# A hybrid decoder layer on one core: the residual sum ahead of the second-norm scaling, and x chunks projected in three pieces instead of four

## The chip, the cores and the metric

The kernel runs on one core of a Trainium2 chip. The metric is the device time of one execution in microseconds; before the change the median of three runs was 953.03 us (952.98 to 953.38). The engines of the core are TensorE (PE, its weight loads shown apart as PEld), VectorE (DVE), ScalarE (ACT), GpSimd (POOL) and SyncE (SP), each with its own queue of instructions. DMA transfers are issued from the queues of SP and POOL.

## What is computed

One layer, 1024 tokens with 16 meta tokens in front (1040 columns), model width 1024, FFN width 4096. The reference, cut:

```python
u = rmsnorm(h, g_pre_mix)
q, k, v, x_rec, y_rec = split(u @ w_in)       # 512, 128, 128, 512, 512
a_out = rg_lru(conv4(x_rec)) * gelu(y_rec)    # 8 blocks of 64, gates r and i
b_out = window_attention_with_sinks(q, k, v)  # 8 heads, window 128
h = h + rmsnorm(concat(b_out, a_out) @ w_out, g_post_mix)
f = rmsnorm(h, g_pre_ffn)
h = h + rmsnorm(relu(f @ w_ff1)**2 @ w_ff2, g_post_ffn)
```

In `rg_lru` two gates per channel come from block-diagonal 64x64 matrices: `r = sigmoid(x w_a + b_a)`, `i = sigmoid(x w_x + b_x)`, then `a = exp(-8 r softplus(-lam))`, and `h_t = a_t h_(t-1) + sqrt(1 - a_t^2) i_t x_t` over the tokens.

## The kernel before

Channels lie on the 128 partitions and tokens along the free axis until the output projection, where tokens turn to the partitions. Every float32 product is made of two rounded halves: `split` takes the high part on ACT (L96; on DVE, L98, when it is told to) and the low part on DVE (L99), and `mm3` (L125, L130, L131) issues three matmuls, high x high, high x low, low x high. The FFN, from about 345 us on, uses a scheme with fewer block products; the change does not touch it.

The instructions of each engine stand in an order that a scheduler fixes when the kernel is built: it follows the order of the program with priorities, and `behind(name, ins)` adds an order (no semaphore) between two instructions of one engine. `deferred` lowers the priority of what it encloses.

The stretches that matter here, in time:

- **Attention with fills, about 90 to 190 us.** Two passes of four quarters make scores (L628, L632 into `ps_s`), a softmax, transposes (L678 into `ps_pt`) and the product with v (L696 into `ps_o`). Between them PE is filled with projections of the remaining weight chunks, in the order x0, q2, x1, q3, x2, x3, y0, y1, then y2 and y3. `project(w, pieces, sink)` takes a piece of columns at a time: a bank `ps_acc` (there are two), 24 matmuls (8 k-slices x 3), then `sink`. For x the pieces are `ALL`, four of 272, 256, 256 and 256 columns, and the sink is an ACT copy (L490). For q and y they are `REAL2`, two of 512; the y sink is a DVE copy (L751). A convolution (`conv`) follows each x chunk.
- **Gates.** `gates(c)`, for the four chunks c of 128 channels: for three column pieces of 348, 348 and 344, six matmuls with 64 rows (L818): three for r and i each, on the upper and the lower 64 rows, into banks of `ps_s`, `ps_pt` or `ps_o`. ACT then takes the sigmoids (L82). `gather` (L832 to L835, with a copy on POOL, L833) brings the halves together.
- **Recurrence.** `decay` (exponential and tanh on ACT), `recur` (square root on ACT, two DVE products L850 and L851, a DVE scan L852), gelu of y on ACT, and `rec_out` (DVE product L857 and the split). It goes for chunks 0 and 1 first, then for 2 and 3. `load_wo` and `split_wo` bring the rows of `w_out` in between. The y projection gives PE work meanwhile.
- **Output projection, from about 226 us.** `out_mm(t, po, kcs)` for eight token tiles t of 128, two banks of 512 columns, k-slices kc 0 to 3 (attention), 4 and 5 (chunks 0 and 1), 6 and 7 (chunks 2 and 3). For tiles 0 to 3 the slices are taken in three rounds (0 to 3 for all, 4 and 5 for all, then 6 and 7 tile by tile); tiles 4 to 7 take all eight at once.
- **Norms of a tile.** `out_norm(t, po)`: sums of squares on ACT, the factor on POOL (L176), the scaling with the gain on DVE, DVE residual sum `h + xr` (L954), a DMA of h to the output, sum of squares on ACT, a second factor on POOL, and a DVE scaling into `xr` (L959). `u2_tiles` (L971 transposes on PE into `ps_o`, evictions L976 on DVE and L982 on ACT) makes the FFN's input from `xr`; it is called for tile 0 when t is 4.

Of the kernel before, what the change touches and what calls it, by code (L numbers as in the profile page):

```python
# [12 lines left out]
ALU = mybir.AluOpType  # L13
# [24 lines left out]
def hybrid_layer(  # L38
# [6 lines left out]
    nc = tc.nc  # L45
# [12 lines left out]
    def slot(tag, shape, dt=F32):  # L58
        uid[0] += 1
        return slab.tile(shape, dt, tag=tag, name=f"{tag}{uid[0]}", bufs=bufs[tag])  # L60

    def pair(tag, shape):
        return slot(tag, shape, F32R), slot(tag, shape, F32R)

    def bank(tag, shape=(P, 512)):
        uid[0] += 1
        return ps.tile(list(shape), F32, tag=tag, name=f"ps_{tag}{uid[0]}")
# [26 lines left out]
    def split(hi, lo, src, eng=None):  # L94
        if eng is None:
            nc.scalar.copy(hi, src)  # L96
        else:
            eng.tensor_copy(hi, src)  # L98
        low = nc.vector.tensor_tensor(lo, src, f32(hi), op=ALU.subtract).ins  # L99
        mark[0] = low.name  # L100
        return low
# [4 lines left out]
    def behind(name, *inss):  # L106
        for ins in inss:
            tc.add_manual_dep(
                ins, name,
                mybir.DependencyInfo(  # L110
                    mybir.DependencyClass.NoSync, mybir.DependencyReason.DATA
                ),
                reason="order",
            )
# [8 lines left out]
    def mm3(dst, lhs, rhs, start, stop, after=None):  # L123
        (lh, ll), (rh, rl) = lhs, rhs
        ins = nc.tensor.matmul(  # L125
            dst, lh, rh, start=start, stop=False, skip_group_check=True
        ).ins
        if after:
            behind(after, ins)
        nc.tensor.matmul(dst, lh, rl, start=False, stop=False, skip_group_check=True)  # L130
        last_mm[0] = nc.tensor.matmul(  # L131
            dst, ll, rh, start=False, stop=stop, skip_group_check=True
        ).ins.name
# [33 lines left out]
    def rstd_of(ssq_parts, n=P):  # L167
        ms = small.tile([P, 1], F32, name="ms", tag="ms")
        if len(ssq_parts) == 1:
            nc.gpsimd.tensor_scalar(ms[:n], ssq_parts[0], EPS, None, op0=ALU.add)  # L170
        else:
            nc.vector.scalar_tensor_tensor(
                ms[:n], ssq_parts[0], EPS, ssq_parts[1], op0=ALU.add, op1=ALU.add
            )
        rs = small.tile([P, 1], F32, name="rs", tag="rs")
        last_pow[0] = nc.gpsimd.tensor_tensor(  # L176
            rs[:n], ms[:n], half_pow[:n], op=ALU.pow
        ).ins.name
        return rs[:n]
# [85 lines left out]
    def project(w, pieces, sink):  # L265
        wh, wl = w
        for t0, n in pieces:
            acc = bank("acc")
            for kc in range(KC):
                uh, ul = u[kc]  # L270
                mm3(
                    acc[:, :n], (wh[:, kc, :], wl[:, kc, :]),
                    (uh[:, t0 : t0 + n], ul[:, t0 : t0 + n]),
                    kc == 0, kc == KC - 1,
                )
            sink(acc[:, :n], t0, n)
# [10 lines left out]

    ALL = [(0, 272), (272, 256), (528, 256), (784, 256)]
    REAL2 = [(16, 512), (528, 512)]

# [175 lines left out]
    def new_q():  # L468

        q = pair("b", [P, T])  # L470

        def sink_q(acc, t0, n):
            c = slice(t0 - NMETA, t0 - NMETA + n)
            for h in range(2):
                r = HALF[h]
                nc.scalar.activation(q[h][r, c], acc[r], AF.Copy, scale=-(HD ** -0.5))
            for h in range(2):
                r, o = HALF[h], HALF[1 - h]
                nc.vector.scalar_tensor_tensor(  # L479
                    q[h][o, c], acc[r], -(HD ** -0.5), f32(q[h][r, c]),  # L480
                    op0=ALU.mult, op1=ALU.subtract,
                )

        return q, sink_q

    def new_x(tag="d"):
        xr = slot(tag, [P, TT])

        def sink_x(acc, t0, n):
            nc.scalar.copy(xr[:, t0 : t0 + n], acc)  # L490

        return xr, sink_x
# [224 lines left out]
    def conv(c, xr, tag="d"):  # L717
        y = slot(tag, [P, TT])
        nc.vector.tensor_scalar(
            y, xr, prm[:, c, 3:4], prm[:, c, 4:5], op0=ALU.mult, op1=ALU.add  # L720
        )
        for k in (2, 1, 0):
            s = 3 - k
            nc.vector.scalar_tensor_tensor(
                y[:, s:], xr[:, : TT - s], prm[:, c, k : k + 1], y[:, s:],
                op0=ALU.mult, op1=ALU.add,
            )
        xc[c] = y
# [3 lines left out]
    def fill_q(j):  # L732
        def run(w):
            q, sink = new_q()
            project(w, REAL2, sink)
            qs[j] = q
        return run

    def fill_x(c):
        def run(w):  # L740
            xr, sink = new_x()
            project(w, ALL, sink)
            conv(c, xr, "b" if c == 3 else "d")
        return run

    def fill_y(c):
        def run(w):
# [5 lines left out]

            project(w, REAL2, sink)
            ys[c] = y
# [49 lines left out]
    def gates(c):  # L805
        ch, cl = pair("b", [P, TT])
        split(ch, cl, xc[c])


        z = [slot("c", [P, TT]) for _ in range(2)]  # L810
        for t0, n in ((0, 348), (348, 348), (696, 344)):
            acc = []
            for s in range(2):
                flip[0] += 1
                acc.append(bank(("s", "pt", "o")[flip[0] % 3]))
            for k, (a, b) in enumerate(((0, ch), (0, cl), (1, ch))):
                for s in range(2):
                    nc.tensor.matmul(  # L818
                        acc[s][:, :n], gw[HALF[s], a, c, :], b[HALF[s], t0 : t0 + n],
                        start=k == 0, stop=k == 2, skip_group_check=True,  # L820
                    )
            for s in range(2):
                lut(
                    z[s][:, t0 : t0 + n], acc[s][:, :n], AF.Sigmoid,
                    bias=prm[:, c, 5 + s : 6 + s],
                )
        rg[c] = z
# [106 lines left out]
    def out_banks(t):  # L934
        tag = ("pt", "o", "acc", "s", "pt", "acc", "s", "pt")[t]
        return [bank(tag), bank(tag)]

    def out_norm(t, po):
        xr = slot("d", [P, D])
        nc.sync.dma_start(xr, x[t * P : (t + 1) * P, :])  # L940
        h = slot("raw", [P, D])
        ssq = [small.tile([P, 1], F32, name=f"sq{n}", tag=f"sq{n}") for n in range(2)]
        for n in range(2):
            c = slice(512 * n, 512 * n + 512)
            nc.scalar.activation(
                h[:, c], po[n], AF.Square, scale=RMS_SC, accum_out=ssq[n]
            )
        rs = rstd_of(ssq)
        for n in range(2):
            c = slice(512 * n, 512 * n + 512)  # L950
            nc.vector.scalar_tensor_tensor(
                h[:, c], po[n], rs, gmix_b[:, c], op0=ALU.mult, op1=ALU.mult
            )
        nc.vector.tensor_tensor(h, h, xr, op=ALU.add)  # L954
        nc.sync.dma_start(out[t * P : (t + 1) * P, :], h)
        ssq2 = small.tile([P, 1], F32, name="ssq", tag="ssq")
        nc.scalar.activation(xr, h, AF.Square, scale=RMS_SC, accum_out=ssq2)
        rs2 = rstd_of([ssq2])
        nc.vector.tensor_scalar(xr, h, rs2, None, op0=ALU.mult)  # L959
        return xr  # L960

    def u2_tiles(t, xn):
# [36 lines left out]
    def operand(tiles):  # L999
        pairs = []  # L1000
        for t_ in tiles:
            hi, lo = pair("b", [P, 2, 512])
            split(hi, lo, t_)
            pairs.append((hi, lo))
        return pairs
# [90 lines left out]
        out_mm(t, pos[t], range(4))  # L1096
    for t in range(4):
        out_mm(t, pos[t], range(4, 6))
    xns = {}
    wa, ya = {}, {}  # L1100
    ESH = [P, 2, 4, P]

# [10 lines left out]
    for t in range(8):  # L1113
        po = pos[t] if t < 4 else out_banks(t)
        out_mm(t, po, range(6 if t < 4 else 0, KC))
        for t_ in {4: (0,), 5: (2,), 6: (4,), 7: (5,)}.get(t, ()):
            u2_tiles(t_, xns[t_])
        xns[t] = out_norm(t, po)
        for t_ in {4: (1,), 5: (3,), 7: (6,)}.get(t, ()):
            u2_tiles(t_, xns[t_])  # L1120
        if t == 4:
            a11_early.update(early(0, 0, pair("a", ESH)))
        if t == 5:
            b11 = operand(u2f[0][0:2])
            a12_early.update(early(1, 0, pair("ws", ESH)))
        if t == 6:
            b21 = operand(u2f[0][2:4])
            hl = slot("b", ESH, F32R), slot("e", ESH, F32R)
            a11_early.update(early(0, 2, hl))
# [382 lines left out]
```

## Time and profile before

| | |
|---|---|
| median of 3 runs | 953.03 us |
| profiled execution | 953.59 us |
| its span in the trace | 951.9 us |
| PE busy | 941.2 us, 4712 matmuls |
| DVE busy | 659.2 us |
| ACT busy | 508.2 us |
| POOL busy | 131.4 us |
| mean granted clock of PE | 0.998 |

The busy times are sums over one profiled execution; the chip ran it once with the profiler on. A line of the timeline gives the start in us from the beginning of the span, the duration, the engine, the source line, the operation, output and inputs by their names, the shapes, and the number of equal instructions put together on the line. What stands in brackets at the end is the idle time of the engine just before and what ended it. Matmuls overlap in a pipeline, so their recorded durations are longer than the distance from one start to the next; that distance is what one costs.

### The profile page before, as it was taken

The page shows a single profiled execution, that of the slowest core. Times are in us where ns is not written, and L with a number is a line of the kernel's source. Part 1 is how long each engine was busy: PE and PEld are TensorE (multiplying, and loading weights), DVE is VectorE, ACT ScalarE, POOL GpSimd, SP SyncE. Part 2 cuts the span into 40 slices and gives each one's busy share as a digit, 9 for nine tenths or more (in the row PEclk, how much of TensorE's full clock was granted, in tenths as well). Part 3 has the DMA queues.
Part 4 walks back from the last instruction along what each step waited for, and adds up shares of the span by engine and source line. Part 5 has one row for each costly group of instructions (what it writes and reads, how often), then busy time and mean ns, then how long its engine had stood idle before and what let it go on. Part 6 is the DMA issues. An engine that isn't in the chain of part 4 may idle for free.

```text
span 951.9 us, 12417 instructions
## 1 busy us (share of the span) xinstructions
PE 941.2 (99%) x4712; PEld 787.7 (83%) x4712; DVE 659.2 (69%) x849; ACT 508.2 (53%) x858; POOL 131.4 (14%) x205
## 2 busy tenths in 40 slices
PE   9999999999999999999999999999999999999996
PEld 8999999877888878888888888888888888888885
DVE  6667798879855887665644465476667676769883
ACT  8546766568644564443555575653533343445441
POOL 4104546410021100010000000000121000001201
PEclk9999999999999999999999999999999999999999
DMA  8220011104225468674432354334777765647934
GB/s 272 57 67 23 24 45 42 49 23 128 79 108 174 153 206 280 199 230 145 166 101 88 111 193 127 102 111 131 190 165 179 200 194 180 197 133 201 242 65 89
DMA packets 88199, 130.21 MB, mean 137 GB/s; under 512 B 13702, under 2 KB 52630, under 8 KB 88140
## 3 DMA queue, kind: packets, MB, share of 16 engines
q1 hardware_dynamic: 78972, 104.44, 34.3%
q0 software_dynamic: 8880, 24.19, 12.2%
q8 instruction: 37, 0.61, 0.3%
q10 hardware_dynamic: 288, 0.79, 0.2%
q14 instruction: 22, 0.18, 0.1%
HBM read 109.93 MB, written 18.87 MB: 135 GB/s over the span
## 4 chain that ended last, share of the span: by engine, by line
PE 86%; DVE 7%; ACT 3%; issue 2%; DMA 2%; SPq 0%; DVEq 0%; POOL 0%; ACTq 0%
PE ps_acc L125 10%; PE ps_acc L131 10%; PE ps_acc L130 10%; PE ps_s L131 6%; PE ps_s L125 6%; PE ps_s L130 6%; PE ps_pt L130 6%; PE ps_pt L131 6%; PE ps_pt L125 6%; PE ps_o L131 5%; PE ps_o L130 5%; PE ps_o L125 5%; ACT c L82 1%; PE ps_o L696 1%; PE ps_acc L282 1%
## 5 line engine op out<-in xcount | busy, mean ns | idle before, releaser
L99 DVE TENSOR_TENSOR ws<-raw,ws 128x1024 fp32r<-128x1024 f32 (+1 forms) x69 | 82.6, 1198 | 71.2 <-ACT ws L96 24.6
L96 ACT CAST ws<-raw 128x1024 fp32r<-128x1024 f32 (+1 forms) x68 | 69.7, 1025 | 90.9 <-PE ps_o L130 33.6
L125 PE MATMUL ps_acc<-a,ws 128*128 128x256 f32 (+2 forms) x272 | 88.5, 326 | 0.7 <-DVE b L479 0.4
L96 ACT CAST ws<-e 128x1024 fp32r<-128x1024 f32 x41 | 43.0, 1050 | 85.1 <-PE ps_o L130 37.6
L130 PE MATMUL ps_acc<-a,ws 128*128 128x256 f32 (+2 forms) x272 | 87.8, 323 | 0.0
L131 PE MATMUL ps_acc<-a,ws 128*128 128x256 f32 (+2 forms) x272 | 87.5, 322 | 0.0
L99 DVE TENSOR_TENSOR b<-b,b 128x1024 fp32r<-128x1024 f32 (+2 forms) x50 | 58.9, 1178 | 27.6 <-PE ps_o L130 22.4
L96 ACT CAST b<-b 128x1024 fp32r<-128x1024 f32 (+2 forms) x49 | 50.0, 1020 | 41.0 <-DVE b L997 35.5
L99 DVE TENSOR_TENSOR ws<-e,ws 128x1024 fp32r<-128x1024 f32 x41 | 50.1, 1223 | 30.7 <-ACT ws L96 17.3
L683 POOL TENSOR_SCALAR_AFFINE_SELECT c<-c 128x512 fp32r<-128x512 f32 x64 | 55.5, 883 | 68.9 <-ACT c L96 54.9
L125 PEld LDWEIGHTS ps_acc<-a,ws 128*128 128x128 f32 x272 | 51.3, 189 | 5.5 <-issue 0.9
L131 PEld LDWEIGHTS ps_acc<-a,ws 128*128 128x128 f32 x272 | 51.2, 188 | 4.0 <-issue 0.2
L130 PEld LDWEIGHTS ps_acc<-a,ws 128*128 128x128 f32 x272 | 51.1, 188 | 3.6 <-issue 0.2
L125 PE MATMUL ps_acc<-ws,b 128*128 128x512 f32 (+1 forms) x120 | 46.3, 387 | 0.0
L131 PE MATMUL ps_acc<-ws,b 128*128 128x512 f32 (+1 forms) x120 | 46.2, 385 | 0.0
L130 PE MATMUL ps_acc<-ws,b 128*128 128x512 f32 (+1 forms) x120 | 46.0, 384 | 0.0
L125 PE MATMUL ps_pt<-ws,b 128*128 128x512 f32 x112 | 44.2, 395 | 0.0
L131 PE MATMUL ps_pt<-ws,b 128*128 128x512 f32 x112 | 44.1, 394 | 0.0
L130 PE MATMUL ps_pt<-ws,b 128*128 128x512 f32 x112 | 44.0, 393 | 0.0
L125 PE MATMUL ps_s<-ws,b 128*128 128x512 f32 x110 | 43.4, 395 | 0.0
L130 PE MATMUL ps_s<-ws,b 128*128 128x512 f32 x110 | 43.4, 394 | 0.0
L131 PE MATMUL ps_s<-ws,b 128*128 128x512 f32 x110 | 43.2, 393 | 0.0
(415 smaller groups left out, 2660.6 us busy)
## 6 DMA issues: line engine op xcount, KB each, us to landing
raw<-in_w_ff_dram SPq DMA_DIRECT2D x59, 512.0 KB, 3.5
e<-in_w_ff_dram SPq DMA_DIRECT2D x43, 512.0 KB, 3.9
a<-in_w_ff_dram SPq DMA_DIRECT2D x12, 512.0 KB, 5.9
s_dram<-a POOLq DMA_DIRECT2D x12, 512.0 KB, 4.0
raw<-in_w_in_dram SPq DMA_DIRECT2D x9, 512.0 KB, 3.7
c<-in_x_dram SPq DMA_DIRECT2D x8, 512.0 KB, 4.9
d<-in_x_dram SPq DMA_DIRECT2D x8, 512.0 KB, 4.6
out_dram<-raw SPq DMA_DIRECT2D x8, 512.0 KB
```

What stands on the lines that cost most here:

```text
L82: ins = nc.scalar.activation(*args, **kwargs).ins
L96: nc.scalar.copy(hi, src)
L99: low = nc.vector.tensor_tensor(lo, src, f32(hi), op=ALU.subtract).ins
L125: ins = nc.tensor.matmul(dst, lh, rh, start=start, stop=False, skip_group_check=True).ins
L130: nc.tensor.matmul(dst, lh, rl, start=False, stop=False, skip_group_check=True)
L131: last_mm[0] = nc.tensor.matmul(dst, ll, rh, start=False, stop=stop, skip_group_check=True).ins.name
L282: last_mm[0] = nc.tensor.matmul(acc[:, :n], w[k // 2][:, kc, :], u[kc][k % 2][:, t0 : t0 + n], start=k == 0 and kc == 0, stop=k == last an ...
L683: nc.gpsimd.affine_select(out=p_[:, :, s], in_=f32(p_[:, :, 0]), pattern=[[0, 4], [g, P]], compare_op=op, fill=0.0, base=0, channel_multip ...
L696: nc.tensor.matmul(two[:, :, oc : oc + w], v, p_.rearrange("p (j i) s c -> p j (i s c)", j=2)[:, :, pc : pc + w], start=n == 0 and k == 0, ...
```

## The change

Two edits. In the first, `out_norm` ends with the second factor and a new function `out_scale` does the scaling. For tiles 0 to 2 the scaling is placed behind the residual sum of the next tile. A table `scale_at` says after which tile's `out_norm` each scaling is issued: tile 0 after tile 1, tile 1 after 2, tiles 2 and 3 after 3, and from tile 4 on after their own. In the second, the x chunks are projected in `THIRDS`, three pieces of 348, 348 and 344 columns, in place of `ALL`; the gates use the same three pieces as before, now by that name. An x chunk then has 72 matmuls where it had 96, and three ACT copies where it had four.

```diff
+    THIRDS = [(0, 348), (348, 348), (696, 344)]
...
     def fill_x(c):
         def run(w):
             xr, sink = new_x()
-            project(w, ALL, sink)
+            project(w, THIRDS, sink)
             conv(c, xr, "b" if c == 3 else "d")
...
-        for t0, n in ((0, 348), (348, 348), (696, 344)):
+        for t0, n in THIRDS:
...
+    summed = {}
+
     def out_norm(t, po):
...
-        nc.vector.tensor_tensor(h, h, xr, op=ALU.add)
+        summed[t] = nc.vector.tensor_tensor(h, h, xr, op=ALU.add).ins.name
         nc.sync.dma_start(out[t * P : (t + 1) * P, :], h)
         ssq2 = small.tile([P, 1], F32, name="ssq", tag="ssq")
         nc.scalar.activation(xr, h, AF.Square, scale=RMS_SC, accum_out=ssq2)
-        rs2 = rstd_of([ssq2])
-        nc.vector.tensor_scalar(xr, h, rs2, None, op0=ALU.mult)
+        return h, xr, rstd_of([ssq2])
+
+    def out_scale(t, h, xr, rs2):
+        ins = nc.vector.tensor_scalar(xr, h, rs2, None, op0=ALU.mult).ins
+        if t < 3:
+            behind(summed[t + 1], ins)
         return xr
...
-    xns = {}
+    xns, halfway = {}, {}
+    scale_at = ((), (0,), (1,), (2, 3), (4,), (5,), (6,), (7,))
...
-        xns[t] = out_norm(t, po)
+        halfway[t] = out_norm(t, po)
+        for k in scale_at[t]:
+            xns[k] = out_scale(k, *halfway.pop(k))
```

The source does not say the order in which the engines issue; the scheduler settles it when the program is built. Built, the changed program has 96 fewer matmuls on PE and 4 fewer copies on ACT. DVE, POOL and SP issue as many instructions as before, SP in the same order. PE, DVE and ACT stand in another order between about 90 us (x chunk 1) and 345 us.

## The prediction

> **What bounds the kernel now.** I read the page from the top: busy time of the engines, then the chain that ended last, then stretches of the span by windows, and at last the timeline of each engine where the change touches it.
>
> ```profile
> span 951.9 us, 12417 instructions
> PE 941.2 (99%) x4712; PEld 787.7 (83%) x4712; DVE 659.2 (69%) x849; ACT 508.2 (53%) x858; POOL 131.4 (14%) x205
> PE 86%; DVE 7%; ACT 3%; issue 2%; DMA 2%; SPq 0%; DVEq 0%; POOL 0%; ACTq 0%
> 95.00:165.00 70.00, 68.96 (x510) 65.15 (x509) 59.96 (x98) 48.09 (x147) 37.04 (x60) 1.00 0.11 31
> 212.00:260.00 48.00, 47.81 (x207) 38.47 (x206) 44.73 (x45) 36.26 (x42) 2.68 (x2) 1.00 0.33 97
> 260.00:345.00 85.00, 85.00 (x403) 69.68 (x402) 57.64 (x89) 46.14 (x103) 12.46 (x25) 1.00 0.50 162
> ```
>
> The last three lines are windows: start and end, length, then busy time and instruction count of PE, weight loads, DVE, ACT and POOL, granted clock, DMA share, GB/s. PE sets the time: 941.2 of 951.9 us, at clock 1.00 in every stretch shown. So an edit counts by what it does to PE's instructions or to PE's few waits. The first part of the change lies in 260 to 345 us, where PE has no idle time; the second in 95 to 212, with its consequences up to 260. The profiled execution took 953.59 us, 1.7 us more than its span and 0.56 us above the median of 953.03. I form a difference on the trace and add it to the median.
>
> **Part one: the next tile's residual sum ahead of the scaling.** No instruction comes or goes. In the before trace:
>
> ```profile
> 268.63 0.75 DVE L959 TENSOR_SCALAR d<-raw,rs 128x1024 f32<-128x1024 f32 x1 [2.12 <-POOL rs L176]
> 270.90 1.23 DVE L954 TENSOR_TENSOR raw<-raw,d 128x1024 f32<-128x1024 f32 x1
> 281.39 1.03 PE L971 MATMUL ps_o<-ident,d 128*128 128x128 f32 x8
> ```
>
> DVE waits 2.12 us for tile 0's factor, scales, and adds tile 1's residual at 270.90. In the order in which the changed program issues, that sum stands first and fills DVE's wait; the scaling follows at about 272. What is queued behind the scaling now is shorter, and what waits for it, tile 0's transposes on PE, comes only at 281.39: over 8 us of cover. For tiles 2 and 3 the scalings slide behind other DVE work, but in the order built they still stand ahead of the transposes that read them, by an estimate of 8 us or more. The orders on SP and POOL are the same but for one swap on POOL. PE has no gap there (85.00 of 85.00), so there is nothing to win either. I take 0; were the cover gone, PE would wait for a 1.23 us sum at most twice, +2.5.
>
> **Part two: x chunks in three pieces. Fewer, longer matmuls.** 24 matmuls per piece: 4 chunks lose 96 matmuls (384 to 288) over the same 1040 columns.
>
> ```profile
> 159.81 0.28 PE L125 MATMUL ps_acc<-a,ws 128*128 128x256 f32 x1
> 162.17 0.28 PE L131 MATMUL ps_acc<-a,ws 128*128 128x256 f32 x1
> 259.16 0.39 PE L125 MATMUL ps_pt<-a,b 128*128 128x512 f32 x1
> 260.31 0.40 PE L131 MATMUL ps_pt<-a,b 128*128 128x512 f32 x1
> ```
>
> There are twenty intervals between the first two rows: 2.36/20 = 0.118 us for 256 columns. Five between the last two: 1.15/5 = 0.230 for 512. That is 0.44 ns a column and about 5 ns fixed per matmul, so 96 x 5 ns = **-0.5 us**. [...] Four ACT copies also go; ACT is 53% busy and PE reads none of them: 0.
>
> **Stalls in 95 to 165 us.** PE alternates here between attention and x pieces, and a piece begins when one of the two `ps_acc` banks is free.
>
> ```profile
> 101.29 0.29 PE L131 MATMUL ps_acc<-a,ws 128*128 128x272 f32 x1
> 102.02 0.35 PE L125 MATMUL ps_acc<-a,ws 128*128 128x256 f32 x1 [0.44 <-DVE b L479]
> 122.19 0.60 PE L678 MATMUL ps_pt<-ident,c 128*128 128x128 f32 x4
> 122.55 1.46 PE L696 MATMUL ps_o<-c,b 128*128 128x256 f32 x6
> 157.43 0.60 PE L678 MATMUL ps_pt<-ident,c 128*128 128x128 f32 x4
> 158.33 0.39 PE L628 MATMUL ps_s<-b,b 128*128 128x256 f32 x1 [0.30 <-DVE c L646]
> 158.79 0.28 PE L632 MATMUL ps_s<-b,b 128*128 128x256 f32 x1
> 159.35 0.39 PE L125 MATMUL ps_acc<-a,ws 128*128 128x256 f32 x1 [0.29 <-ACT d L490]
> ```
>
> By starts: 101.29 to 102.02 is 0.73 for a matmul of about 0.12, so 0.61 lost. 157.43 to 158.33 is 0.90 for four transposes that take 0.36 at 122.19: 0.54 lost. 158.79 to 159.35: 0.56 for 0.118, 0.44 lost. Together 1.6; smaller hitches in the same stretch I put at 0.2 (the window shows 1.04 idle, without the tails that are modelled as busy). In the changed program's order, with 12 pieces instead of 16, each of these consumers stands further behind its producer, and I found no new pair that is closer. I take **-1.8**; the ends are 0 (the same waits elsewhere, since DVE is 59.96 of 70 busy) and -2.0.
>
> **Gates cut into more runs.** Gate matmuls have 64 rows and go in pairs on two row halves. Where such a run meets 128-row matmuls, time is lost:
>
> ```profile
> 197.84 0.40 PE L131 MATMUL ps_acc<-a,ws 128*128 128x512 f32 x1
> 198.16 0.73 PE L818 MATMUL ps_o<-b,e 64*128 64x344 f32 x3
> 198.82 0.50 PE L125 MATMUL ps_acc<-a,ws 128*128 128x512 f32 x1
> 208.83 0.39 PE L131 MATMUL ps_acc<-a,ws 128*128 128x512 f32 x1
> 209.14 0.42 PE L818 MATMUL ps_s<-b,e 64*128 64x348 f32 x1
> 210.53 0.32 PE L818 MATMUL ps_o<-b,e 64*128 64x344 f32 x1
> 210.78 0.50 PE L125 MATMUL ps_acc<-a,ws 128*128 128x512 f32 x1
> ```
>
> The trio: 197.84 to 198.82 is 0.98, less 0.23 for the first matmul, so 0.75. Its fuller half has two matmuls of 344 columns (0.157 each by the pitch above), 0.31, and 0.43 is left. The run of 18 (209.14 to 210.78): 208.83 to 210.78 is 1.95, less 0.23, less 9 x 0.157 = 1.41, and 0.31 is left. So a run costs about 0.37 us beside its matmuls. Before, the 72 gate matmuls form 6 runs (5, 10, 3, 18, 18, 18; 37 in the fuller halves). In the changed order they form 9 (3, 1, 3, 5, 3, 24, 18, 3, 12; 39). That is 3 x 0.37 + 2 x 0.157 = **+1.4**, ends 1.2 and 2.1. [...]
>
> **Cover taken from the recurrence.** The gates feed a long chain on ACT and DVE: sigmoids, decay, square root, scan, products, hi/lo split, and its last half feeds kc 7 of the output projection. Before, 63 matmuls of the y projection (512 columns) follow the last gate; in the changed order 49. The 14 others move ahead of the gates, which costs PE nothing by itself but takes 14 x 0.230 = 3.2 us of cover.
>
> ```profile
> 232.63 0.40 PE L131 MATMUL ps_o<-a,b 128*128 128x512 f32 x1
> 233.21 0.50 PE L130 MATMUL ps_pt<-a,b 128*128 128x512 f32 x1 [0.19 <-DVE a L99]
> 258.03 0.68 DVE L99 TENSOR_TENSOR b<-d,b 128x512 fp32r<-128x512 f32 x1
> ```
>
> The low part that PE needs for kc 7 is ready at 258.03 + 0.68 = 258.71, and its first reader is the matmul at 260.31: 1.6 us of slack. The chain itself, from the last gate:
>
> ```profile
> 212.15 0.58 ACT L82 ACTIVATE c<-ps_o,prm 128x344 f32<-128x344 f32 x1
> 224.62 0.68 DVE L751 COPY d<-ps_acc 128x512 f32<-128x512 f32 x1
> 228.60 1.20 DVE L99 TENSOR_TENSOR a<-raw,a 128x1024 fp32r<-128x1024 f32 x1
> 233.17 1.05 ACT L96 CAST a<-raw 128x1024 fp32r<-128x1024 f32 x1 [3.87 <-DMA raw<-in_w_out_dram]
> 240.18 1.03 ACT L96 CAST a<-raw 128x1024 fp32r<-128x1024 f32 x1
> 241.56 1.22 DVE L99 TENSOR_TENSOR a<-raw,a 128x1024 fp32r<-128x1024 f32 x1
> 243.59 2.04 ACT L82 ACTIVATE c<-c 128x1040 f32<-128x1040 f32 x2
> 244.76 2.39 DVE L850 SCALAR_TENSOR_TENSOR c<-b,c 128x1040 f32<-128x1040 f32 x2 [1.39 <-ACT c L82]
> ```
>
> In the changed order: the last gate's run is shorter, so its last sigmoid ends about 0.5 sooner after it; the y copy at 224.62 (0.68) partly leaves the stretch before the split at 228.60, which frees the buffer for the load that ACT awaits at 233.17, about -0.3; the cast at 240.18 moves behind the square root at 243.59, -0.95; its DVE split, at 241.56 before, then stands inside the last stretch, +1.1; one more half split (0.68) stands ahead of the last one, +0.6. Together -0.05: the chain is as long as it was after the last gate. PE arrives 3.2 us sooner by the lost cover, and 0.4 more if the hitch at 232.63 to 233.21 (0.58 for a matmul of 0.23) goes, since the weights' split is then early. So 3.6 - 1.6 = 2.0 us of a new wait at kc 7, ends 0 (the chain finds 2 us more) and 2.6. Net with the lost hitch: **+1.6**.
>
> **Sum.** -0.5 - 1.8 + 1.4 + 2.0 - 0.4 = +0.7 on the trace (953.59 to 954.3). On the median: 953.03 + 0.7, rounded to **953.8**. Past 345 us the two orders are the same.
>
> **Rivals.** *The tail is not late*: the load that ACT awaits 3.87 us for comes enough sooner, or DVE catches up (44.73 of 48 busy, so there are only 3 us to find). Then the 2.0 goes: -1.3, 951.7. For it: four of five terms of the chain are readings of order, not of time. Against it: DVE's share. *Runs of gates cost nothing extra where PE would have waited anyway, with the tail not late*: -1.3 - 1.4 = -2.7, about 950.3. It needs the 0.37 to be shared with a wait that I did not see. *The stalls stay*, the one on the slower side: the pieces of 348 columns keep a bank longer, the `ps_acc` pair is still released by a DVE that is 86% busy (59.96 of 70), and the first reader of each freed bank waits as long as now. Decided by whether DVE lags behind the order by more than one piece (24 x 0.157 = 3.8 us). Then +1.8: 953.03 + 2.5 = 955.6. With that, tail at its upper end 0.6 more, 956.2. *The change does not do what it says* is no case here for part two, as its instruction counts differ; for part one it would be the same 0.
>
> **How the numbers follow.** Forecast 0.49 (953.0 to 954.8); tail not late 0.20 (951.0 to 952.6); cheap runs and no tail 0.08; stalls stay 0.23 (955 to 956.4). The range 951.0 to 956.4 leaves out the cheap case and a little on each side, some 0.15. A measurement of this kernel can tell about 0.2%, 1.9 us, from no change: 951.1 and 954.9 are the bounds. Faster 0.10 (the cheap case and the lowest edge of the tail case); slower 0.29 (stalls stay, and the forecast's upper edge with a late tail of 2.6); the same 0.61.
>
> **What would show it.** Right: 288 matmuls with 348 or 344 columns at about 0.158 us; no wait of PE over 0.3 us between 95 and 165; nine runs of gates at about 0.37 each; one wait of about 2 us on DVE L99 at kc 7 of the first token tile; no idle PE from there to 345. Wrong: the waits of 95 to 165 back under other names, PE waiting on the scaling's reader (L971), no wait at kc 7, or a difference that arises after 345 us.

## The result and the profile after

The changed kernel takes 958.38 us (median of six runs, 957.26 to 959.19), the kernel before 953.0. The ratio is 1.0057, with a 95% interval of 1.0046 to 1.0067: 0.57% slower, where 953.8 was forecast with 956.4 as the upper end. A second series on another occasion gave 958.95 (956.42 to 960.09) against 953.68, ratio 1.0050 (1.0039 to 1.0062).

Two rows of the page and five windows of the changed kernel's profiled execution, which took 959.19 us. The last three columns of a window are PE's granted clock, the DMA share and GB/s.

```profile
span 957.2 us, 12224 instructions
PE 945.4 (99%) x4616; PEld 790.6 (83%) x4616; DVE 657.4 (69%) x849; ACT 507.9 (53%) x854; POOL 131.4 (14%) x205
95.00:165.00 70.00, 70.00 (x445) 66.33 (x444) 56.95 (x93) 46.47 (x135) 33.92 (x59) 1.00 0.13 39
212.00:260.00 48.00, 47.29 (x209) 37.62 (x208) 42.92 (x42) 36.63 (x43) 3.00 (x2) 1.00 0.29 88
260.00:345.00 85.00, 83.30 (x381) 68.15 (x382) 56.87 (x87) 44.40 (x102) 11.30 (x25) 0.96 0.46 152
262.40:268.10 5.70, 5.67 (x13) 4.47 (x14) 1.39 (x3) 1.38 (x4) 0.56 (x1) 0.50 0.29 95
261.60:268.40 6.80, 5.97 (x14) 4.72 (x15) 2.49 (x6) 1.38 (x4) 0.56 (x1) 0.50 0.29 99
```

PE has 96 matmuls fewer and is busy 4.2 us longer. In 95 to 165 us it has no idle time any more (70.00 of 70, before 68.96). The loss lies where the window of 260 to 345 shows two things that it did not show before: 1.7 us of idle time (another 0.7 lies in the window before it, where there was 0.2), and a clock of 0.96. The last two rows have the cause of the 0.96: the clock stood at 0.50. By the clock record of the trace it did so from 261.58 to 268.41, for 6.83 us. PE's timeline there:

```profile
258.82 0.49 PE L131 MATMUL ps_pt<-a,b 128*128 128x512 f32 x1
260.68 0.50 PE L125 MATMUL ps_pt<-a,b 128*128 128x512 f32 x1 [1.36 <-ACT b L96]
261.01 0.40 PE L130 MATMUL ps_pt<-a,b 128*128 128x512 f32 x1
262.43 0.80 PE L131 MATMUL ps_pt<-a,b 128*128 128x512 f32 x1 [1.02 <-DVE b L99]
263.03 0.63 PE L125 MATMUL ps_pt<-a,b 128*128 128x512 f32 x1
263.45 0.63 PE L130 MATMUL ps_pt<-a,b 128*128 128x512 f32 x1
267.72 0.63 PE L131 MATMUL ps_o<-a,b 128*128 128x512 f32 x1
268.15 0.52 PE L125 MATMUL ps_o<-a,b 128*128 128x512 f32 x1
268.50 0.40 PE L130 MATMUL ps_o<-a,b 128*128 128x512 f32 x1
```

These are kc 6 (up to 258.82) and kc 7 of the first token tile. PE waits for the high part of the recurrence's last half (258.82 to 260.68 is 1.86 for a matmul of 0.23, 1.63 lost) and again for the low part (261.01 to 262.43, 1.19 lost). The clock fell during this second wait. Behind it the matmuls of 512 columns stand 0.42 to 0.43 us apart (263.03 to 263.45) until 268.15, and at 0.23 from 268.50 on.

The two traces laid on each other, by matmuls counted from the end of the program, where the orders are equal. The shift is that of the changed kernel, with the 0.4 us taken off by which it was already ahead at 19 us, where the two programs are still the same (matmuls of 512 columns stand 0.43 us apart at the start of both; that ended at 5.58 us here and at 6.45 before):

| place in the trace of before | changed kernel later by |
|---|---|
| 252 us, ahead of kc 6 and 7 | -0.54 us |
| 268 us, in the second tile's part | +5.34 us |
| 376 us | +5.21 us |
| 944 us, last matmul | +5.76 us |

So the change is 0.5 us ahead until the output projection, and loses 5.9 us within some ten us.

### The profile page after: what moved, and what is told of

The parts are those of the page before. It is cut to its first block, busy times and chain, and to the rows that moved or that the text cites. A ratio compares the mean times of both kernels' runs of the same rounds, so it can differ in the third digit from the quotient of the medians.

```text
span 957.2 us, 12224 instructions
## 1 busy us (share of the span) xinstructions
PE 945.4 (99%) x4616; PEld 790.6 (83%) x4616; DVE 657.4 (69%) x849; ACT 507.9 (53%) x854; POOL 131.4 (14%) x205
## 3 DMA queue, kind: packets, MB, share of 16 engines
q1 hardware_dynamic: 78972, 104.44, 33.4%
## 4 chain that ended last, share of the span: by engine, by line
PE 92%; DVE 3%; ACT 2%; issue 1%; DMA 1%; SPq 0%; DVEq 0%; ACTq 0%
PE ps_acc L125 11%; PE ps_acc L130 11%; PE ps_acc L131 11%; PE ps_pt L131 6%; PE ps_s L131 6%; PE ps_pt L125 6%; PE ps_s L125 6%; PE ps_pt L130 6%; PE ps_s L130 6%; PE ps_o L125 5%; PE ps_o L130 5%; PE ps_o L131 5%; PE ps_o L697 2%; PE ps_acc L282 1%; PE ps_s L629 1%
## 5 line engine op out<-in xcount | busy, mean ns | idle before, releaser
L130 PE MATMUL ps_acc<-a,ws 128*128 128x512 f32 (+3 forms) x240 | 82.9, 346 | 0.0
L125 PE MATMUL ps_acc<-a,ws 128*128 128x512 f32 (+3 forms) x240 | 82.9, 346 | 0.0
L131 PE MATMUL ps_acc<-a,ws 128*128 128x512 f32 (+3 forms) x240 | 82.2, 343 | 0.0
L684 POOL TENSOR_SCALAR_AFFINE_SELECT c<-c 128x512 fp32r<-128x512 f32 x64 | 53.3, 847 | 75.3 <-ACT c L96 65.8
L125 PEld LDWEIGHTS ps_acc<-a,ws 128*128 128x128 f32 x240 | 45.2, 189 | 4.3 <-issue 0.7
L131 PEld LDWEIGHTS ps_acc<-a,ws 128*128 128x128 f32 x240 | 45.2, 188 | 3.7 <-issue 0.2
L130 PEld LDWEIGHTS ps_acc<-a,ws 128*128 128x128 f32 x240 | 45.2, 188 | 3.6 <-issue 0.4
```

The source lines that it names most:

```text
L125: ins = nc.tensor.matmul(dst, lh, rh, start=start, stop=False, skip_group_check=True).ins
L131: last_mm[0] = nc.tensor.matmul(dst, ll, rh, start=False, stop=stop, skip_group_check=True).ins.name
L684: nc.gpsimd.affine_select(out=p_[:, :, s], in_=f32(p_[:, :, 0]), pattern=[[0, 4], [g, P]], compare_op=op, fill=0.0, base=0, channel_multip ...
```

## Experiments

**Each edit alone.** The first kernel has `project(w, ALL, sink)` again; the second is the kernel before with only this:

```diff
-            project(w, ALL, sink)
+            project(w, THIRDS, sink)
```

> Only the first edit: the next tile's residual sum ahead of the scaling; x stays in four pieces. PE's order up to the output projection is that of before. Theory (the loss is a wait of PE for the recurrence at kc 7 of the first token tile, and the slow clock behind it, both brought by the x pieces): 953.0, within 0.5 of before, no half-speed matmuls after the start. Rival (the moved sum and scaling are at fault, since the loss shows in the window of 260 to 345 us where they lie): 957 to 958, and PE waits there.

> Only the second edit: x in three pieces, the norms as before. Theory: 958.4 as the whole change, within 0.7, with the same wait of 2.8 us at kc 7 and about a dozen matmuls of 0.43 us behind it. Rival (the moved sum is at fault): about 952, 0.9 below before.

The first edit alone: 953.11 against 952.8, ratio 1.0001 (0.9991 to 1.0010). Windows of it:

```profile
95.00:165.00 70.00, 68.98 (x512) 65.21 (x511) 59.94 (x98) 48.05 (x147) 36.58 (x60) 1.00 0.11 32
260.00:345.00 85.00, 85.00 (x403) 69.89 (x402) 58.34 (x89) 45.80 (x103) 11.29 (x25) 1.00 0.48 161
```

PE is busy all the time from 260 to 345, as before. The rival that the moved sum is at fault is out, though the loss shows in its window. The second edit alone: 956.59 against 952.8, ratio 1.0039 (1.0024 to 1.0054). It waits as the whole change does (shift -0.48 at 252 us, +2.75 at 268), but its profiled execution had a granted clock of 0.998, where the changed kernel's had 0.995. The 958.4 that was expected was a miss; the runs below take it up.

**Extra work in the wait.** Token tile 0's first bank is accumulated from kc 0 to 5 in one piece, just ahead of kc 6; its first 12 (or 6) matmuls have then been done once already for nothing:

```diff
...
     for t in range(4):
+        if t == 0:
+            out_mm(t, pos[t], range(4), (0,))    # range(2) in the second kernel
+            out_mm(t, pos[t], range(4), (1,))
+            continue
         out_mm(t, pos[t], range(4))
     for t in range(4):
-        out_mm(t, pos[t], range(4, 6))
+        out_mm(t, pos[t], range(4, 6), (1,) if t == 0 else (0, 1))
...
+        if t == 0:
+            out_mm(t, po, range(6), (0,))
         out_mm(t, po, range(6 if t < 4 else 0, KC))
```

> The whole change, and 12 matmuls more: the first 12 accumulations of token tile 0's first bank are done a second time, just ahead of kc 6 and 7. 12 x 0.23 = 2.76 us of PE work that fill the wait of 2.8 us. Theory (idle time of about 2.5 us within a few us drops the clock to half, and that costs 2.6 us beside the wait): 955.8, faster than the changed kernel in spite of more work, no matmul at 0.43 us. Rival (the slow clock does not depend on the idle time): 958.4, half speed still there. If the recurrence is delayed by the extra work: over 959.

> The whole change with 6 repeated matmuls (1.38 us) ahead of kc 6 and 7 of tile 0, in place of 12. The wait left is about 1.4 us. Theory: the wait and the extra work together are the same 2.8 us; if half of the idle time is still enough to drop the clock, 957 to 958.4, if not, 955.8 as with 12. Rival (slow clock unrelated to idle time): 958.4.

With 12 matmuls more: 955.92 (955.67 to 956.51) against 952.8. The same 260 to 345 us window:

```profile
260.00:345.00 85.00, 85.00 (x402) 69.80 (x401) 58.75 (x92) 45.75 (x104) 11.33 (x25) 1.00 0.48 164
```

No wait, clock 1.00, and 2.5 us less than the changed kernel in spite of 2.76 us more work: the extra work takes just the place of the wait, and the slow clock is gone. With 6 more: 955.41 against 953.49. Here the reading is less clean than the edit. The chain to chunk 3's first low part (product, then low split) was shorter as well:

```profile
258.46 0.69 DVE L858 TENSOR_TENSOR d<-d,c 128x512 f32<-128x512 f32 x1
260.87 0.69 DVE L99 TENSOR_TENSOR b<-d,b 128x512 fp32r<-128x512 f32 x1
261.61 0.50 PE L131 MATMUL ps_pt<-a,b 128*128 128x512 f32 x1
```

The low part was ready at 260.87 + 0.69 = 261.56, 47.5 us after the first matmul behind the last gate (214.07; the changed kernel has 49.1), and its reader started at 261.61. Only some 0.05 us was lost, so the run says nothing on a wait of half the length. Of the 1.6 us, 1.0 was saved ahead of DVE's last stretch, and 0.6 by one low split fewer ahead of this one on DVE. So the order of DVE is worth something, and that is used below.

**The cover alone, on the kernel before.** x in four pieces, norms as before, only the projection of y chunk 2 written ahead of chunk 3's gates:

```diff
     for c in range(NLRU):
+        if c == 3:
+            next_fill()
         gates(c)
         if c < 2:
             gather(c)
-    next_fill()
```

> The kernel before, x in four pieces and the norms untouched, with the projection of y chunk 2 written ahead of the gates of chunk 3: in PE's order 48 y matmuls follow the last gate in place of 63, and nothing else changes in the number of instructions. Theory (the lost cover makes the loss, whatever the x pieces): a wait of 15 x 0.23 - 1.6 = 1.9 us at kc 7, so 954.5 if the clock holds and 956 to 957 if it drops. Rival (the three pieces or the gate runs make the loss): 953.0.

It took 957.38 (956.55 to 958.43) against 953.49, ratio 1.0042 (1.0028 to 1.0056). Its profiled execution, of 956.7 us:

```profile
259.94 0.39 PE L130 MATMUL ps_pt<-a,b 128*128 128x512 f32 x1
261.36 0.50 PE L131 MATMUL ps_pt<-a,b 128*128 128x512 f32 x1 [1.03 <-DVE b L99]
261.93 0.40 PE L130 MATMUL ps_pt<-a,b 128*128 128x512 f32 x1
263.17 0.50 PE L131 MATMUL ps_pt<-a,b 128*128 128x512 f32 x1 [0.84 <-DVE b L99]
```

Two waits: 1.42 - 0.23 = 1.19 and 1.24 - 0.23 = 1.01 us, and a granted clock of 0.998 in this execution. Two of its four times, though, are 958.05 and 958.43, the second with a granted clock of 0.996. The loss can be had without the pieces of 348 columns. What makes it is y work on the wrong side of the gates.

**By chance or by kernel.** The changed kernel and the second edit alone, once more, side by side:

> The changed kernel once more, beside the one with the second edit alone, to see whether the slow clock belongs to the kernel or comes by chance. Six times of it lay from 957.3 to 959.2, four of the other from 955.5 to 957.8, though PE's wait is the same 2.8 us in both traces. Theory (the wait is long enough that the clock drops in some executions and not in others, by where the wait falls): both kernels spread from 955.5 to 959.2, the medians within 1 us of each other. Rival (the first edit brings the slow clock): this one stays at 958 or more, the other at 956.6.

> The second edit alone once more. Theory: as the whole change, times from 955.5 to 959.2, some with a granted clock of 0.998 and some with 0.995 to 0.997. Rival (the first edit brings the slow clock): all at 956 to 957 with 0.998.

The changed kernel: 956.42, 956.95, 958.48, 959.41, 959.61, 960.09, with granted clocks of 0.998 and 0.997 for the first two, 0.996 for the third and 0.995 for the last three. The second edit alone: 955.96 and 956.19 at 0.998, 958.04, 958.50 and 958.96 at 0.996. Medians 958.95 and 958.04. Both kernels have executions with and without the slow clock, so it does not belong to the first edit. The profiled execution of the changed kernel is this time one without:

```profile
258.93 0.43 PE L131 MATMUL ps_pt<-a,b 128*128 128x512 f32 x1
260.71 0.50 PE L125 MATMUL ps_pt<-a,b 128*128 128x512 f32 x1 [1.36 <-ACT b L96]
261.05 0.40 PE L130 MATMUL ps_pt<-a,b 128*128 128x512 f32 x1
262.47 0.50 PE L131 MATMUL ps_pt<-a,b 128*128 128x512 f32 x1 [1.03 <-DVE b L99]
262.81 0.40 PE L125 MATMUL ps_pt<-a,b 128*128 128x512 f32 x1
262.40:268.10 5.70, 5.63 (x24) 4.62 (x25) 2.81 (x6) 2.75 (x8) 0.56 (x1) 1.00 0.27 96
```

The waits are the same to within 0.1 us; behind them 24 matmuls start in the 5.7 us in which the other execution started 13, and the clock is 1.00. This execution is shifted by +2.42 at 268 us instead of +5.34. The wait costs 2.9 us, and the slow clock, when it comes, up to 2.9 more.

The clock records say a little on the chance. In the traces of the two kernels the stretches between two changes of the clock are 942.08 us before, and 256.0, 6.83 and 686.08 us after the change: 276, 75, 2 and 201 times 3.413 us. Cut the changed kernel's first execution into such stretches: in the one that ends where the clock fell, 258.17 to 261.58, PE was busy for 1.88 us. Whether it matters where the waits fall in these stretches is not shown: ahead of PE's last matmul there is a single fall.

**Taking the wait away.** Two mends on the changed kernel. One holds the second half of y chunk 2 (from its fourth k-slice) and all of chunk 3 behind the last gate matmul:

```diff
-            project(w, REAL2, sink)
+            project(w, REAL2, sink, {2: (1, 3), 3: (0, 0)}.get(c))
...
                     kc == 0, kc == KC - 1,
+                    last_gate[0] if hold == (i, kc) else None,
```

The other keeps the products of the second token half off DVE until chunk 3's first half is split:

```diff
...
+        if half:
+            behind(half0_low[0], ins)
         ah, al = at[half][2 + c // 2]
-        split(ah[:, c % 2, :], al[:, c % 2, :], y, eng)
+        low = split(ah[:, c % 2, :], al[:, c % 2, :], y, eng)
+        if not half:
+            half0_low[0] = low.name
```

> The whole change, and the second half of y chunk 2 from its fourth k-slice on and all of y chunk 3 held behind the last gate matmul, so that 63 y matmuls cover the recurrence as in the kernel before (49 in the changed one). Gates now form 7 runs in place of 9. Theory: no wait at kc 7 over 0.5 us, no half speed, 951.5 to 952.5 (the 0.9 us that the changed kernel is ahead at 245 us stays, and two runs of gates fewer may give 0.7). Rival (the slow clock has a reason of its own that comes with the three pieces): 955 to 956, half speed still there. A miss of another kind: PE waits for the gates' input, as it may no longer run y ahead of them, about 953 to 954.

> The whole change, and the recurrence's products and low splits of the second token half placed behind the low split of chunk 3's first half on DVE: only half 0 is needed by kc 6 and 7 of the first tile. In the changed kernel four products of 0.65 us and three splits of 0.6 that PE does not wait for stand ahead. Theory (the loss is only the wait and the slow clock behind it): ready about 3 us sooner, no wait over 0.5 us, no half speed, 952.5 (at 256 us the changed kernel is about 0.5 us ahead). Rival (nine runs of gates, or something past 345 us, cost time too): 954 or more with no wait at kc 7.

> Both mends at once: 63 y matmuls behind the last gate matmul and half 0 first on DVE. The run with the y matmuls alone still waited 1.45 us at kc 7. Theory: no wait, 952.2, some 0.6 below before. Rival (the wait at kc 7 moves to another input, such as the high parts on ACT or the weights of kc 6): 953 to 954.

The y matmuls alone: 954.22 against 952.8, ratio 1.0018 (1.0008 to 1.0027), a miss by about 2 us. A wait was left:

```profile
259.20 0.39 PE L130 MATMUL ps_pt<-a,b 128*128 128x512 f32 x1
260.43 0.50 PE L131 MATMUL ps_pt<-a,b 128*128 128x512 f32 x1 [0.85 <-DVE b L99]
235.64 1.05 ACT L96 CAST a<-d 128x1024 fp32r<-128x1024 f32 x1 [4.48 <-DMA d<-in_w_out_dram]
```

1.23 - 0.23 = 1.0 us here and 0.4 just before. The gates ended 3.4 us sooner (the first matmul behind them starts at 209.84 in place of 213.28), but DVE's last stretch began at 246.44, hardly sooner than the 246.69 of the changed kernel: ACT waited 4.48 us for the next load of weights. And DVE still did the second half's products ahead of what PE waits for. Half 0 first, alone: 954.21 against 953.49, ratio 1.0009 (1.0000 to 1.0018), with this left:

```profile
258.98 0.40 PE L131 MATMUL ps_pt<-a,b 128*128 128x512 f32 x1
259.84 0.50 PE L125 MATMUL ps_pt<-a,b 128*128 128x512 f32 x1 [0.47 <-ACT b L96]
```

Some 0.6 us, now for the high part, so 2 us of the wait are gone, and the slow clock with it: the granted clock of all eleven times is 0.997 to 0.999. Both together: 953.44 against 953.49, ratio 0.9999 (0.9991 to 1.0008), PE without idle time from 212 to 345:

```profile
212.00:260.00 48.00, 48.00 (x210) 39.05 (x209) 43.48 (x43) 35.51 (x41) 3.00 (x2) 1.00 0.31 88
260.00:345.00 85.00, 85.00 (x403) 69.85 (x402) 61.37 (x95) 46.46 (x105) 11.29 (x25) 1.00 0.51 168
```

That settles the cause of the loss; the 952.2 that was expected did not come. Its trace is 0.85 us ahead at 252 us and only 0.47 at the end, and it spends 2.0 us outside the span where the kernel before spends 1.7. Neither difference was traced to a cause.

**The runs of gates.** On top of both mends, the gate matmuls each behind the one before, in the order of the source:

```diff
-                    nc.tensor.matmul(
+                    ins = nc.tensor.matmul(
...
+                    ).ins
+                    if last_gate[0]:
+                        behind(last_gate[0], ins)
+                    last_gate[0] = ins.name
```

> The version with both mends (63 y matmuls behind the last gate, half 0 first), and the 72 gate matmuls kept in the order of the source, which makes 6 runs (2, 3, 1, 7, 29, 30) in place of 7 with the two row halves alternating. In the version without it the long runs of 24 and 33 cost 0.8 and 1.3 us beside their matmuls. If that comes of halves that don't alternate: 0.45 + 0.8 + 1.3 - 2 x 0.3 = 1.9 less, 951.5 to 952. Rival (in runs over 18 PE waits for the sigmoids to free the six banks, about 0.43 us each): 953.4, unchanged.

952.16 (951.44 to 953.18) against 953.68, ratio 0.9985 (0.9977 to 0.9994): the only version faster than the kernel before, by 1.5 us. The time came close to what was expected, but little of it for the reason given: in its long runs the rival was right. Two neighbouring gate starts in the run of 29, a pause, and the sigmoid that ended it:

```profile
201.82 0.40 PE L822 MATMUL ps_pt<-b,e 64*128 64x344 f32 x1
201.83 0.32 PE L822 MATMUL ps_s<-b,e 64*128 64x348 f32 x1
202.24 0.42 PE L822 MATMUL ps_o<-b,e 64*128 64x344 f32 x1
201.62 0.56 ACT L82 ACTIVATE c<-ps_o,prm 128x344 f32<-128x344 f32 x1
```

From 201.83 to 202.24 there are 0.41 us where 0.16 is the pitch; there are four such pauses in the two long runs (0.41 and 0.44, then 0.30 and 0.44), the first of each after 18 or 19 matmuls. The gates have six banks, three matmuls to a bank, and a sigmoid must free one before the next three: the one above ends at 202.18. The gates take 9.93 us all told, against 10.66 in the version without the chain, where 1.9 less was expected. That explains some 0.5 us on the trace at 252 us (1.36 ahead, not 0.85). The rest of the 1.3 us between the two versions lies past 345 us and outside the span, in the two differences that stay open.

## Why the prediction was wrong, step by step

**Part one at zero: right**, by the first experiment. One detail was wrong. In the changed kernel DVE still waits for POOL:

```profile
273.11 1.41 DVE L954 SCALAR_TENSOR_TENSOR raw<-ps_o,rs,e 128x512 f32<-128x512 f32 x2 [2.37 <-POOL rs L176]
275.70 0.75 DVE L964 TENSOR_SCALAR d<-raw,rs 128x1024 f32<-128x1024 f32 x1
286.28 1.03 PE L978 MATMUL ps_o<-ident,d 128*128 128x128 f32 x8
```

The wait of 2.37 us now stands ahead of tile 1's scaling with the gain; the sum did not fill it. The cover held: 275.70 + 0.75 to 286.28 are 10 us.

**Fewer matmuls (-0.5) and stalls (-1.8): right.** All three stalls of 95 to 165 us are gone. The hitch at the weights' split only shrank (-0.2, where -0.4 was put). With the shift at 252 us, -0.54 = fewer - 1.8 + 2.1 - 0.2, and the fewer matmuls brought about 0.6.

**Runs of gates (+1.4): too small, +2.1**, the upper end. Counted as in the prediction, with the 0.1 us that the first matmul behind a run also loses, six runs took 8.6 us and nine take 10.7. The run of 24 is the largest miss:

```profile
201.00 0.40 PE L131 MATMUL ps_acc<-a,ws 128*128 128x512 f32 x1
203.20 0.74 PE L819 MATMUL ps_s<-b,e 64*128 64x348 f32 x3
203.89 0.51 PE L125 MATMUL ps_acc<-a,ws 128*128 128x512 f32 x1
```

2.89 - 0.23 - 12 x 0.157 = 0.78 beside its matmuls, where 0.37 was put for every run: it outruns its six banks (ACT's sigmoid that frees `ps_s` runs until 203.14), and its last three stand alone on one half.

**The new wait at kc 7 (2.0, ends 0 and 2.6): place and mechanism right, size 2.8 to 2.9.** The first step that failed is "the chain is as long as it was after the last gate". It was 1.2 us longer:

```profile
213.28 0.50 PE L131 MATMUL ps_acc<-a,ws 128*128 128x512 f32 x1
231.28 0.35 SPq L871 DMA_DIRECT2D raw<-in_w_out_dram  x1
235.90 1.05 ACT L96 CAST a<-raw 128x1024 fp32r<-128x1024 f32 x1 [4.55 <-DMA raw<-in_w_out_dram]
246.69 1.24 DVE L851 SCALAR_TENSOR_TENSOR c<-b,c 128x1040 f32<-128x1040 f32 x1 [1.69 <-ACT c L82]
261.69 0.69 DVE L99 TENSOR_TENSOR b<-d,b 128x512 fp32r<-128x512 f32 x1
```

From the first matmul behind the last gate, the low part is ready after 262.38 - 213.28 = 49.1 us (before 258.71 - 210.78 = 47.9). DVE's last stretch grew by 1.7 as forecast (246.69 to 262.38 is 15.7; 244.76 to 258.71 was 13.95). What did not come is the 1.8 us that the steps ahead of it were to save; they saved 0.6 (246.69 - 213.28 = 33.4 against 34.0). The weights' load was indeed issued sooner after the gates, at 18.0 us in place of 19.05, but its cast began 4.62 us after the issue, in place of 3.34. So ACT's wait for it grew from 3.87 to 4.55. I had moved the issue and taken the transfer's time as fixed. The issue before, and the DMA queues during the load (packets, MB, share of the 16 engines), from 229 to 234 us before and from 231 to 236 us in the changed kernel:

```profile
229.83 0.35 SPq L870 DMA_DIRECT2D raw<-in_w_out_dram  x1
q1 hardware_dynamic: 144, 0.52, 33.0%
q1 hardware_dynamic: 144, 0.52, 31.5%
q8 instruction: 1, 0.02, 1.2%
```

The load is the same; what is new is one packet of 16 KB of the queue that the profile calls "instruction". It started at 233.66, 2.38 us after the issue, and took 0.93 us; in the trace of before none started between 229 and 236 us. No run moved the packet by itself: that it makes the transfer longer is a guess from these two traces.

**The second step that failed, and the larger: the clock, up to 2.9 us, was put at nothing.** I priced idle time of PE at its own length. The trace of before had matmuls at half speed, at the start of the program:

```profile
1.50:5.50 4.00, 3.98 (x9) 3.15 (x10) 0.31 (x1) 2.24 (x5) 3.03 (x8) 1.00 0.80 259
```

Nine matmuls of 512 columns in 4 us, 0.44 each, though the clock column has 1.00 there: the trace's clock record begins only at 6.45 us, where the half speed ends. That trace does not show that idle time brings the half speed. Still, half speed behind a new wait belonged in the rival with a late tail and in the upper bound, as a chance. In the changed kernel's trace two waits of 1.6 and 1.2 us, with two matmuls between, went with a clock of 0.50, and it fell before the second had ended. By their times and mean clocks that happened in ten of twelve executions (957.26 to 960.09 us at 0.995 to 0.997), though one trace alone shows it.

**The rivals.** "The stalls stay" had the right sign and the wrong place: the stalls went. The tail that is not late was the opposite of what came. By the terms as measured, -0.6 - 1.8 + 2.1 - 0.2 + 2.9 = +2.4 without the slow clock and up to +5.3 with it; the 0.4 us of creep past 345 us and 0.3 outside the span, neither traced to a cause, come on top. Of the 4.9 us between the 954.3 forecast for the trace and 959.19, 2.9 are the slow clock, 0.9 the longer wait and 0.7 the runs of gates.

## What to carry to other kernels

Work that a scheduler moves from behind a point to the front of it costs nothing where it lands and everything at the place that it covered: count what stands between a chain's start and its reader, and reckon the chain with its transfers, which need not keep their time: this one took 3.34 us from issue to cast before and 4.62 after. On a PE that was busy for 99% of the span, a new wait of 2.9 us cost up to twice its length here, since in one trace the clock stood at 0.50 for 6.83 us: price both. A little useless work in the wait was then faster than the wait. Look in the queue of the late engine for work that nobody waits for: half 0 first gave back 2 of the 2.9 us.

## What the runs showed of the hardware

With idle time of 2.8 us in two pieces within 3.6 us, PE's clock stood at 0.50 for 6.83 us in one execution, from before the second piece had ended, and at 1.00 from 260 to 345 us in another of the same kernel with the same waits. Of twelve times of the changed kernel two have no sign of it (956.42 and 956.95); ten lie from 957.26 to 960.09, at mean clocks of 0.995 to 0.997. With a wait of 1.0 and 0.4 us one of ten executions stood out (956.64 at a clock of 0.997, the others 953.56 to 954.89). With none, the granted clock of all runs was 0.997 to 0.999. A load of 512 KB of weights took 3.34 us from issue to use before the change and 4.62 after, where an instruction packet of 16 KB started 2.38 us behind the issue. A run of 64-row matmuls cost 0.3 to 0.5 us beside its matmuls for lengths of 1 to 18 (0.78 for 24), and another 0.1 at the first full-height matmul behind it, which took 0.34 us where 0.23 is the pitch.
